# Hybrid encoder step on one core: a norm row spread by TensorE, partial sums of squares added in PSUM, half factors written directly, and a longer planned delay for two w_o loads

## Chip, cores and metric

The kernel runs on one core of one Trainium2 chip. The metric is the device time of one execution in microseconds (us); the figure quoted is the median of several runs.

## The reference

One layer of a streaming encoder for 1024 prompt frames and 32 sample frames (1056 in all), width 1024:

```
h = rmsnorm(x, g_norm);  z = h @ w_in                  # 1024 x 8192
o_a = differential attention(q, k, v of z);  o_r = retention(q, k, v of z)
x = x + (sigmoid(g_a) * o_a + sigmoid(g_r) * o_r) @ w_o          # 1024 x 1024
x = x + (silu(h2 @ w_ff_gate) * (h2 @ w_ff_up)) @ w_ff_down      # h2 = rmsnorm(x), d_ff = 2816
x = x + sigmoid(rmsnorm(x) @ w_ple_gate) * (p @ w_ple)
```

All large products are computed from two f16 parts per operand (a high and a low part, three matmuls per product), so each weight block has to be scaled by a power of two and split into its parts on the chip before TensorE can use it.

## The kernel before

**Stages.** First the eight heads: for each head two weight pairs (A and B, each made of two 256-column blocks of w_in), and for each of nine row tiles of 128 frames a projection, attention and retention (functions `project`, `unit_a`, `unit_b`). Then the product with w_o, the second norm, and the gate/up products over 22 blocks of 128 columns (`load_gu`, `gu_pair`, `gu_sums`), which use a seven-product scheme. Then the down projection (`load_dn`, later `load_dn_now`) and the last gate.

**Order of the work.** A planner (`Flow`) runs at build time. Generators yield estimated costs per engine (M is TensorE, V VectorE, S ScalarE, G GpSimd, D the DMA), waits and delays; the planner simulates the engines by these estimates and emits instructions in the order of its simulated times. On the chip each engine then works through its own list strictly in that order. An estimate changes nothing about an instruction, only its place in the lists. The planner has no view of the real times.

**A weight block's scale.** `load_block_steps` (w_in, w_o), `load_gu` and `load_dn` load a block into a staging tile. For the blocks concerned here, ScalarE squares it in two instructions (L416, L1615, L1668), each leaving one sum per partition; VectorE adds the two sums into a bf16 tile `wamh` (L430, L1619, L1671); TensorE adds over the partitions with a matrix of ones (one column, L300, in `weight_scale`); VectorE makes the scale `s` (L230, L234, L315, L317) and the un-scale `d` (L323). ScalarE and VectorE then write the two parts (L462 and L464; L1587 and L1590). For gate/up blocks VectorE also writes a column of `rf` (L1624) and half of `d`, `hd` (L1626), which the tanh in `gu_out` reads as its scale.

**The start.** `const_a` loads the gain columns, `const_c` the identity and ones matrices, `norm_x(i)` row tile i of x, `load_w(0, 0, ...)` the first two weight blocks, each in four pieces, and `const_g` the norm gains `gb`, already repeated over 128 partitions in DRAM (512 KB). `norm_x` multiplies x by its row factor and by `gb` (L683), after which TensorE transposes the tile (L693) and it is split into two f16 parts `xh`. The first projection (L719 to L721) needs tile 0 and both weight blocks. All loads are issued from the SP queue.

**w_o.** Two blocks come through `load_wo_0`, two through `load_wo_1`, which passes `late`; after each load the planner adds a fixed delay of 3.0 us before the block's reductions.

Of the kernel before, what the change touches and what calls it, by code (L numbers as in the profile page):

```python
# [11 lines left out]
F32 = mybir.dt.float32  # L12
# [37 lines left out]
def _f(x):  # L50
    return float(x)
# [7 lines left out]
def V(n, f=1.0, x=0.0):  # L59
    return {"V": 0.07 + x + f * n / 960.0}  # L60


def S(n, x=0.0):
    return {"S": 0.1 + x + n / 1200.0}
# [6 lines left out]
def M(us):  # L71
    return {"M": us}


def DM(mb):
    return {"D": mb * 2.9}
# [107 lines left out]
def kernel(  # L184
# [38 lines left out]
    def sm(n, tag, bufs=2, dt=F32):  # L223
        return small.tile([P, n], dt, tag=tag, name=tag, bufs=bufs)
# [61 lines left out]
        nc.tensor.matmul(out=pt[:, P:P + n], lhsT=ones32[0:n], rhs=row, start=True, stop=True)  # L286
        return pt[:, P:P + n]

    def weight_scale(amax, n, gi, tag, pool=True, norm=False, total=False, at_bank=None):


        p2 = sm(n, tag + "p2", 3)
        if total:
            if at_bank is None:
                yield ("wait", "id")
            key, psum = at_bank or ("o", ps_o)
            yield ("get", key)
            yield M(0.06)
            ps = psum.tile([P, 512], F32, tag=key, name="mt")[:, 0:1]
            nc.tensor.matmul(out=ps, lhsT=ones16, rhs=amax, start=True, stop=True)  # L300
            yield ("delay", 0.3 if at_bank else 0.0)
            yield from p2of(p2, ps, n, tag, norm)
            yield ("put", key)
        elif pool:
            yield G(0, 0.1)
            ar = sm(n, tag + "ar", 3)
            nc.gpsimd.partition_all_reduce(ar, amax, P, ABSMAX)
            yield from p2of(p2, ar, n, tag)
        else:
            ar = yield from spread_max(amax, n, tag, at_bank)  # L310
            yield from p2of(p2, ar, n, tag, norm)
            yield ("put", at_bank[0] if at_bank else "o")
        yield V(n)
        s = sm(n, tag + "s", 3)
        nc.vector.reciprocal(s, p2)  # L315
        yield V(n, 2.0)
        nc.vector.tensor_scalar(out=s, in0=s, scalar1=_f(2.0 ** (-52 if gi == 1 else -50)) if norm else 16384.0,  # L317
                                scalar2=None, op0=ALU.mult)
        d = sm(n, tag + "d", 6)
        if gi is None:  # L320
            nc.vector.tensor_scalar(out=d, in0=p2, scalar1=_f(2.0 ** (50 if norm else -14)), scalar2=None, op0=ALU.mult)
        else:
            nc.vector.tensor_scalar(out=d, in0=p2, scalar1=gd[:, gi:gi + 1], scalar2=_f(2.0 ** 64) if norm else 1.0,  # L323
                                    op0=ALU.mult, op1=ALU.mult)
        return s, d

# [65 lines left out]
    def load_block_steps(src, w, b, gi, tag, rowf, out, tail=False, due=None, late=None, hold=None):  # L392


        yield ("get", "st")
        st = stage()[:, 0:KD * 256].rearrange("p (k c) -> p k c", k=KD)
        if due == 0:

            for q in range(4):
                yield DM(0.25)  # L400
                nc.sync.dma_start(out=st[:, 2 * q:2 * q + 2], in_=src[:, 2 * q:2 * q + 2])
        else:
            yield DM(1.0)
            nc.sync.dma_start(out=st, in_=src)
            yield ("delay", 3.0)
        norm = rowf is None and not tail
        am4 = sm(4, "wam4", 3)
        am8 = sm(8, "wam8%d" % b, 1) if rowf is not None else None
        for q in range(4):
            if due is not None:  # L410
                yield ("prio", 2 if due - at[0] > FAR else -2)
            sq = st[:, 2 * q:2 * q + 2]
            if norm:
                if q % 2:
                    yield S(1024, 0.24)
                    nc.scalar.activation(w[:, 2 * q - 2:2 * q + 2, 1, 256 * b:256 * b + 256].bitcast(BF16),  # L416
                                         st[:, 2 * q - 2:2 * q + 2], AF.Square, accum_out=am4[:, q // 2:q // 2 + 1])
                continue
            yield V(512)
            if rowf is None:  # L420
                nc.vector.tensor_reduce(out=am4[:, q:q + 1], in_=sq, axis=AX.XY, op=ALU.max, apply_absolute_value=True)
            else:
                nc.vector.tensor_reduce(out=am8[:, 2 * q:2 * q + 2], in_=sq, axis=AX.X, op=ALU.max, apply_absolute_value=True)
        if rowf is not None:
            yield V(8)
            nc.vector.tensor_tensor(out=am8, in0=am8, in1=rowf, op=ALU.mult)
        yield V(4)
        am = sm(1, "wamh" if norm else "wam", 3, BF16 if norm else F32)
        if norm:
            nc.vector.tensor_tensor(out=am, in0=am4[:, 0:1], in1=am4[:, 1:2], op=ALU.add)  # L430
        else:
            nc.vector.tensor_reduce(out=am, in_=am4 if rowf is None else am8, axis=AX.X, op=ALU.max)
        s, d = yield from weight_scale(am, 1, gi, tag + str(b), tail, norm, norm)
        out[b] = d
        if rowf is not None:
            yield V(8)
            sk = sm(KD, "wsk%d" % b, 1)
            nc.vector.tensor_scalar(out=sk, in0=rowf, scalar1=s, scalar2=None, op0=ALU.mult)
        if late is not None:
            w = yield from late()  # L440
        if hold is not None:
            hold.update(st=st, sk=sk)
            return
        yield from split_block(w, b, st, s, None if rowf is None else sk, due)
# [40 lines left out]
    with ExitStack() as pa:  # L485
# [71 lines left out]
        def const_c():  # L557

            yield DM(0.2)
            nc.sync.dma_start(out=cst_sb, in_=cst)  # L560
            yield ("delay", 2.0)
            yield ("set", "id")
            yield ("wait", ("x", 0))
            yield V(P)
            nc.vector.tensor_copy(id16, id32)

        def const_g():

            yield DM(0.5)
            nc.sync.dma_start(out=gb, in_=gbc)  # L570
            yield ("delay", 2.0)
            yield ("set", "gb")

        def const_b():
# [80 lines left out]
        def norm_x(i):  # L655

            R = P if i < NT - 1 else TS
            if i > 2:
                yield ("wait", ("x", i - 3))
            if i > 3:  # L660
# [694 lines left out]
        def stream():  # L1355

            env, wAs, wBs = {}, {0: []}, {}
            flow.add(const_a(), 0)
            flow.add(const_c(), 0)
            flow.add(norm_x(0), 0)  # L1360
            load_w(0, 0, wAs[0], 0, True)
            flow.add(const_g(), 0)
            flow.add(const_b(), 0)
            for i in range(1, NT):
                flow.add(norm_x(i), 0)
# [71 lines left out]
        return psb.tile([P, 512], F32, tag="ps", name="ps")[:, 0:CH]  # L1437

    rf = const.tile([P, NF], F32, name="rf")

# [5 lines left out]
    with ExitStack() as pc:  # L1448
# [18 lines left out]
        with ExitStack() as pw:  # L1467
# [130 lines left out]
            def load_gu(j):  # L1598
# [10 lines left out]
                w = wt[:, 0:n].rearrange("p (i a k c) -> p i a k c", i=7, a=2, k=HK)  # L1609
                tmp = wt[:, n:n + 2 * HK * P].bitcast(F32).rearrange("p (k c) -> p k c", k=HK)  # L1610
                q1, q2, q3, q4 = (st[:, i * HK:(i + 1) * HK, u] for u in range(2) for i in range(2))
                am2 = sm(2, "gam2", 3)
                for i in range(2):
                    yield S(1024, 0.3)
                    nc.scalar.activation(w[:, S3 + i].bitcast(BF16), st[:, i * HK:(i + 1) * HK].rearrange("p k u c -> p u k c"),  # L1615
                                         AF.Square, accum_out=am2[:, i:i + 1])
                yield V(1)
                am = sm(1, "wamh", 3, BF16)
                nc.vector.tensor_tensor(out=am, in0=am2[:, 0:1], in1=am2[:, 1:2], op=ALU.add)  # L1619
                yield ("delay", 1.5)  # L1620
                s, d = yield from weight_scale(am, 1, 1, "gu", norm=True, total=True, at_bank=("ps", psb) if j < 4 else ("ss", pss))

                yield V(1, 1.0, 0.2)
                nc.vector.tensor_scalar(out=rf[:, j:j + 1], in0=d, scalar1=_f(2.0 ** 38), scalar2=d, op0=ALU.mult, op1=ALU.mult)  # L1624
                hd = sm(1, "hdg", 6)
                nc.vector.tensor_scalar(out=hd, in0=d, scalar1=0.5, scalar2=None, op0=ALU.mult)  # L1626
                gus[j] = w, hd
                yield ("set", ("hd", j))
                flow.add(split(j, w, s, A1, q1), 1)
                flow.add(split(j, w, s, A2, q2), 1)  # L1630
# [15 lines left out]
            def load_dn(m):  # L1646

                half = NF // 2
                sts, ams = [], sm(2, "dam", 3)
                yield ("wait", ("hd", NF - 1))  # L1650
                for b in range(2):
                    yield ("get", "st")
                    st = stage()[:, 0:half * P].rearrange("p (j c) -> p j c", j=half)
# [11 lines left out]
                w = wtile().rearrange("p (a j c) -> p a j c", a=3, j=NF)  # L1665
                for b, (st, js) in enumerate(sts):
                    yield S(half * P, 0.3)
                    nc.scalar.activation(w[:, 1, js].bitcast(BF16), st, AF.Square, accum_out=ams[:, b:b + 1])  # L1668
                yield V(2)
                am = sm(1, "wamh", 3, BF16)  # L1670
                nc.vector.tensor_tensor(out=am, in0=ams[:, 0:1], in1=ams[:, 1:2], op=ALU.add)  # L1671
                s, d = yield from weight_scale(am, 1, None, "dn", norm=True, total=True, at_bank=("ss", pss))
                for st, js in sts:
                    yield S(half * P, 0.18)
# [370 lines left out]
```

## Time and profile before

| | |
|---|---|
| median of 3 runs | 1919.94 us (1919.64 to 1921.41) |
| profiled execution, its own time | 1921.23 us |
| its span (first to last instruction) | 1919.5 us |
| granted TensorE clock, mean | 0.996 of 2.4 GHz |
| TensorE busy | 1859.3 us, 97% of the span |
| VectorE busy | 1505.6 us, 78% |
| ScalarE, GpSimd busy | 1085.6 us (57%), 685.8 us (36%) |
| read from and written to HBM | 113.61 MB, 31.34 MB |

Times of single rows are microseconds unless marked ns. In a timeline a row's first figure is when it started, its second how long it took, and the brackets hold the idle time of its engine just before it and what ended that. A matmul's own duration contains its way through the array; in a dense stream the distance between two starts is what one costs.

### The profile page before, as it was taken

The page shows a single profiled execution, that of the slowest core. Times are in us where ns is not written, and L with a number is a line of the kernel's source. Part 1 is how long each engine was busy: PE and PEld are TensorE (multiplying, and loading weights), DVE is VectorE, ACT ScalarE, POOL GpSimd, SP SyncE. Part 2 cuts the span into 40 slices and gives each one's busy share as a digit, 9 for nine tenths or more (in the row PEclk, how much of TensorE's full clock was granted, in tenths as well). Part 3 has the DMA queues.
Part 4 walks back from the last instruction along what each step waited for, and adds up shares of the span by engine and source line. Part 5 has one row for each costly group of instructions (what it writes and reads, how often), then busy time and mean ns, then how long its engine had stood idle before and what let it go on. Part 6 is the DMA issues. An engine that isn't in the chain of part 4 may idle for free.

```text
span 1919.5 us, 38340 instructions
## 1 busy us (share of the span) xinstructions
PE 1859.3 (97%) x14179; PEld 1217.1 (63%) x14179; DVE 1505.6 (78%) x3950; ACT 1085.6 (57%) x2856; POOL 685.8 (36%) x1172
## 2 busy tenths in 40 slices
PE   5899999999999999999999997999999999999999
PEld 3465565555655556655556685777777776666665
DVE  6887788888777787877887589999999986654364
ACT  6777667677676776766656345555655552111132
POOL 2655445444454444544442067232323200000010
PEclk9999999999999999999999999999999999999999
DMA  5222112112021121211214620222121117112031
GB/s 199 70 74 76 63 28 64 57 52 78 18 83 56 32 84 33 77 60 28 84 36 175 234 66 31 101 79 90 56 67 48 63 48 267 61 61 78 12 133 50
DMA packets 71948, 147.43 MB, mean 77 GB/s; under 512 B 25264, under 2 KB 52016, under 8 KB 63824
## 3 DMA queue, kind: packets, MB, share of 16 engines
q1 hardware_dynamic: 71760, 144.98, 22.6%
q8 instruction: 111, 1.82, 0.4%
q14 instruction: 77, 0.63, 0.1%
HBM read 113.61 MB, written 31.34 MB: 76 GB/s over the span
## 4 chain that ended last, share of the span: by engine, by line
PE 72%; DVE 14%; POOL 6%; ACT 4%; issue 2%; DMA 1%; SPq 0%; POOLq 0%; DVEq 0%; ACTq 0%
PE ps L471 9%; PE ps L472 9%; PE ps L473 9%; PE pj L719 7%; PE pj L721 7%; PE pj L720 7%; PE ps L1463 4%; PE ps L1462 4%; PE ps L1461 4%; PE sc L860 1%; PE sc L863 1%; DVE w L464 1%; ACT p L880 1%; DVE nm L870 1%; PE t L909 1%
## 5 line engine op out<-in xcount | busy, mean ns | idle before, releaser
L720 PE MATMUL pj<-w,xh 128*128 128x512 f16 x1024 | 389.5, 380 | 0.0
L719 PE MATMUL pj<-w,xh 128*128 128x512 f16 x1024 | 389.5, 380 | 0.0
L721 PE MATMUL pj<-w,xh 128*128 128x512 f16 x1024 | 389.4, 380 | 0.0
L472 PE MATMUL ps<-mixs,w 128*128 128x352 f16 (+1 forms) x960 | 260.9, 277 | 2.4 <-POOL mixs L1486 2.4
L471 PE MATMUL ps<-mixs,w 128*128 128x352 f16 (+1 forms) x960 | 261.0, 277 | 0.3 <-ACT pws L1339 0.3
L473 PE MATMUL ps<-mixs,w 128*128 128x352 f16 (+1 forms) x960 | 261.0, 277 | 0.0
L471 PEld LDWEIGHTS <-w 128*128 128x128 f16 x1728 | 169.8, 98 | 58.7 <-issue 5.0
L473 PEld LDWEIGHTS <-w 128*128 128x128 f16 x1728 | 169.6, 98 | 56.6 <-issue 5.6
L472 PEld LDWEIGHTS <-w 128*128 128x128 f16 x1728 | 169.6, 98 | 50.4 <-issue 1.5
L721 PEld LDWEIGHTS <-xh 128*128 128x128 f16 x1024 | 100.4, 98 | 121.8 <-issue 1.7
L1595 POOL TENSOR_TENSOR st<-st 128x512 f32<-128x512 f32 x66 | 86.2, 1305 | 250.8 <-DVE w L1590 186.6
L719 PEld LDWEIGHTS <-xh 128*128 128x128 f16 x1024 | 101.5, 99 | 76.0 <-issue 1.7
L720 PEld LDWEIGHTS <-xh 128*128 128x128 f16 x1024 | 100.4, 98 | 73.3 <-issue 1.1
L472 PE MATMUL ps<-tT,w 128*128 128x352 f16 (+1 forms) x528 | 143.6, 277 | 2.9 <-DVE tT L1486 2.9
L880 ACT ACTIVATE p<-sc,nb,scs 128x256 f32<-128x256 f32 (+7 forms) x128 | 106.5, 833 | 69.5 <-POOL nb L872 41.5
L473 PE MATMUL ps<-tT,w 128*128 128x352 f16 (+1 forms) x528 | 143.5, 277 | 0.0
L471 PE MATMUL ps<-tT,w 128*128 128x352 f16 (+1 forms) x528 | 143.5, 277 | 0.0
L1590 DVE SCALAR_TENSOR_TENSOR w<-st,gus,w 128x512 f16<-128x512 f32 x132 | 141.5, 1073 | 0.0
L870 DVE TENSOR_REDUCE nm<-sc 128x1 f32<-128x768 f32 (+6 forms) x112 | 102.9, 918 | 23.4 <-PE sc L863 22.0
L1463 PE MATMUL ps<-a,w 128*128 128x352 f16 x312 | 97.5, 313 | 0.5 <-DVE w L1681 0.5
L1462 PE MATMUL ps<-a,w 128*128 128x352 f16 x312 | 97.5, 313 | 0.0
L1461 PE MATMUL ps<-a,w 128*128 128x352 f16 x312 | 97.5, 312 | 0.0
(428 smaller groups left out, 4872.7 us busy)
## 6 DMA issues: line engine op xcount, KB each, us to landing
st<-in_win_dram SPq DMA_DIRECT2D x30, 1024.0 KB, 4.9
st<-in_wgu_dram SPq DMA_DIRECT2D x22, 1024.0 KB, 4.9
st<-in_wdn_dram SPq DMA_DIRECT2D x16, 704.0 KB, 4.2
out_dram<-kv SPq DMA_DIRECT2D x64, 128.0 KB, 1.7
a_d<-a SPq DMA_DIRECT2D x9, 528.0 KB, 2.7
b<-a_d SPq DMA_DIRECT2D x9, 528.0 KB, 7.4
mixs<-mix_d SPq DMA_DIRECT2D x8, 528.0 KB, 6.6
pw_d<-pws SPq DMA_DIRECT2D x12, 352.0 KB, 5.3
```

The costliest lines, as they stand in the source:

```text
L471: nc.tensor.matmul(out=ps, lhsT=wh, rhs=ah, start=first, stop=False)
L472: nc.tensor.matmul(out=ps, lhsT=wh, rhs=al, start=False, stop=False)
L473: nc.tensor.matmul(out=ps, lhsT=wl, rhs=ah, start=False, stop=last)
L719: nc.tensor.matmul(out=ps, lhsT=xhi, rhs=w[:, k, 0], start=(k == 0), stop=False)
L720: nc.tensor.matmul(out=ps, lhsT=xhi, rhs=w[:, k, 1], start=False, stop=False)
L721: nc.tensor.matmul(out=ps, lhsT=xh[:, k, 1, t0:t0 + P], rhs=w[:, k, 0], start=False, stop=(k == KD - 1))
L870: nc.vector.tensor_reduce(out=nm[0:R, mc], in_=pv, axis=AX.X, op=ALU.max, negate=True)
L880: nc.scalar.activation(pt[0:R, 0:NK], ps[0:R, p0:p0 + NK], AF.Exp, bias=nb[0:R, m:m + 1], scale=sc_ap[0:R], accum_out=Z[0:R, m:m + 1])
L1461: nc.tensor.matmul(out=ps, lhsT=wt[:, 0, j], rhs=a[:, 0, cs], start=(first and j == js[0]), stop=False)
L1462: nc.tensor.matmul(out=ps, lhsT=wt[:, 1, j], rhs=a[:, 0, cs], start=False, stop=False)
L1463: nc.tensor.matmul(out=ps, lhsT=wt[:, 2, j], rhs=a[:, 1, cs], start=False, stop=(last and j == js[-1]))
L1590: nc.vector.scalar_tensor_tensor(out=w[:, i, 1], in0=src, scalar=s, in1=w[:, i, 0], op0=ALU.mult, op1=ALU.subtract)
```

## The change

- `const_g` loads one row of the norm gains (4 KB) instead of 128, and TensorE spreads it over the partitions with two f32 matmuls of 512 columns by a row of ones; ScalarE copies each result into `gb`. It is handed to the planner ahead of `norm_x(0)`.
- The pieces of the second first-head weight block wait for those of the first in the plan, and the x tiles after the first wait for the second block's pieces.
- The VectorE addition of the two partial sums is gone: TensorE takes both as two accumulating one-column matmuls, reading the upper half of each f32 as bf16. This concerns 32 blocks of w_in, 22 of gate/up and 2 of down.
- For gate/up blocks L323 writes half of the un-scale directly into a column of a common tile `hds`; the `rf` columns are computed by one instruction for all 22 blocks, at the first down block, from `hds`.
- After a load that carries `late` (two blocks of w_o) the planned delay is 9.0 us instead of 3.0.

```diff
-            nc.tensor.matmul(out=ps, lhsT=ones16, rhs=amax, start=True, stop=True)
+            top = amax.bitcast(BF16).rearrange("p (c t) -> p c t", t=2)
+            for i in range(2):
+                nc.tensor.matmul(out=ps, lhsT=ones16, rhs=top[:, i:i + 1, 1], start=(i == 0), stop=(i == 1))
...
-        d = sm(n, tag + "d", 6)
+        half = d is not None
+        if not half:
+            d = sm(n, tag + "d", 6)
...
-            nc.vector.tensor_scalar(out=d, in0=p2, scalar1=gd[:, gi:gi + 1], scalar2=_f(2.0 ** 64) if norm else 1.0,
+            nc.vector.tensor_scalar(out=d, in0=p2, scalar1=gd[:, gi:gi + 1], scalar2=_f(2.0 ** (63 if half else 64)) if norm else 1.0,
...
+            if b:
+                yield ("wait", "wl0")
             for q in range(4):
                 yield DM(0.25)
                 nc.sync.dma_start(out=st[:, 2 * q:2 * q + 2], in_=src[:, 2 * q:2 * q + 2])
+            yield ("set", "wl%d" % b)
...
-            yield ("delay", 3.0)
+            yield ("delay", 3.0 if late is None else 9.0)
...
-            nc.vector.tensor_tensor(out=am, in0=am4[:, 0:1], in1=am4[:, 1:2], op=ALU.add)
+            am = am4
...
-            yield DM(0.5)
-            nc.sync.dma_start(out=gb, in_=gbc)
+            yield DM(0.03)
+            nc.sync.dma_start(out=gb[0:1], in_=gbc[0:1])
             yield ("delay", 2.0)
+            yield ("wait", "id")
+            for j in range(2):
+                js = slice(512 * j, 512 * j + 512)
+                yield ("get", "o")
+                yield M(0.9)
+                pt = ps_o.tile([P, 512], F32, tag="o", name="t")
+                nc.tensor.matmul(out=pt, lhsT=ones32[0:1], rhs=gb[0:1, js], start=True, stop=True)
+                yield S(512)
+                nc.scalar.copy(gb[:, js], pt)
+                yield ("put", "o")
...
+            if i:
+                yield ("wait", "wl1")
...
+            flow.add(const_g(), 0)
             flow.add(norm_x(0), 0)
             load_w(0, 0, wAs[0], 0, True)
-            flow.add(const_g(), 0)
...
-                am = sm(1, "wamh", 3, BF16)
-                nc.vector.tensor_tensor(out=am, in0=am2[:, 0:1], in1=am2[:, 1:2], op=ALU.add)
...
-                yield V(1, 1.0, 0.2)
-                nc.vector.tensor_scalar(out=rf[:, j:j + 1], in0=d, scalar1=_f(2.0 ** 38), scalar2=d, op0=ALU.mult, op1=ALU.mult)
-                hd = sm(1, "hdg", 6)
-                nc.vector.tensor_scalar(out=hd, in0=d, scalar1=0.5, scalar2=None, op0=ALU.mult)
-                gus[j] = w, hd
+                gus[j] = w, d
...
-                yield ("wait", ("hd", NF - 1))
+                if m == 0:
+                    yield ("wait", ("hd", NF - 1))
+                    yield V(NF)
+                    nc.vector.scalar_tensor_tensor(out=rf, in0=hds, scalar=_f(2.0 ** 40), in1=hds, op0=ALU.mult, op1=ALU.mult)
```

## Rows read from the trace of the kernel before

**Rows 1.** The page's first part: busy time, share of the span, instructions.
```profile
PE 1859.3 (97%) x14179; PEld 1217.1 (63%) x14179; DVE 1505.6 (78%) x3950; ACT 1085.6 (57%) x2856; POOL 685.8 (36%) x1172
```

**Rows 2.** Windows: length, each engine's busy time, granted clock, DMA share, GB/s.
```profile
0.00:23.30 23.30, 4.08 (x17) 3.14 (x18) 10.73 (x39) 13.76 (x23) 4.43 (x15) 1.00 0.73 247
23.30:75.00 51.70, 44.41 (x235) 23.66 (x232) 46.41 (x122) 35.35 (x92) 32.37 (x57) 0.93 0.40 136
...
1090.00:1250.00 160.00, 144.78 (x1309) 113.03 (x1308) 144.73 (x301) 83.55 (x190) 85.97 (x85) 0.98 0.18 64
1250.00:1600.00 350.00, 350.00 (x3106) 269.19 (x3104) 329.81 (x734) 197.95 (x409) 88.57 (x65) 1.00 0.22 74
```

**Rows 3.** Timeline of the start: begin, duration, engine, line, operation.
```profile
6.61 0.33 SPq L570 DMA_DIRECT2D w<-in_gbc_dram  x1
...
8.23 0.21 DVE L680 TENSOR_SCALAR xrg<-xnr,gsc 128x1 f32<-128x1 f32 x1 [1.27 <-POOL xnr L755]
...
9.22 1.06 ACT L416 ACTIVATE w<-st 128x1024 bf16<-128x1024 f32 x1 [2.15 <-DMA st<-in_win_dram]
...
12.21 1.06 ACT L416 ACTIVATE w<-st 128x1024 bf16<-128x1024 f32 x1 [0.81 <-DMA st<-in_win_dram]
...
14.28 1.28 DVE L683 SCALAR_TENSOR_TENSOR w<-w,xrg 128x1024 f32<-128x1024 f32 x1 [0.72 <-DMA w<-in_gbc_dram]
...
15.62 1.12 PE L693 MATMUL t<-cst_sb,w 128*128 128x128 f32 x4 [1.85 <-DVE w L683]
...
16.24 0.72 ACT L462 ACTIVATE w<-st,A0s 128x512 f16<-128x512 f32 x1 [1.84 <-DVE A0s L317]
...
23.32 0.63 PE L719 MATMUL pj<-w,xh 128*128 128x512 f16 x1
```

**Rows 4.** Copies and casts of line 388: duration ns min/median/max.
```profile
L388 ACT CAST xh<-t x12: 557/585/585, 21.4 to 70.9; 128x512 f16<-128x512 f32 x12
```

**Rows 5.** Waits of TensorE: waiter, releaser, us in total, times, longest.
```profile
PE t L693 <- DVE w L683: 9.4, 4, 4.7
PE mt L300 <- DVE wamh L430: 7.8, 1, 7.8
PE mt L300 <- DVE wamh L1619: 7.2, 5, 3.1
PE ps L472 <- DVE tT L1486: 2.9, 1, 2.9
```

**Rows 6.** Weight loads of line 300: duration ns min/median/max.
```profile
L300 PEld LDWEIGHTS <-cst_sb x56: 96/98/151, 5.8 to 1600.2; 128*128 128x128 bf16 x56
```

**Rows 7.** Timeline of TensorE around one L300 in a dense stretch.
```profile
1297.88 0.31 PE L473 MATMUL ps<-tT,w 128*128 128x352 f16 x1
1298.03 0.17 PE L300 MATMUL mt<-wamh,cst_sb 128*128 128x1 bf16 x1
1298.06 0.24 PE L471 MATMUL ps<-mixs,w 128*128 128x176 f16 x1
```

**Rows 8.** Timeline around two of the five stalls before L300.
```profile
1153.55 0.19 ACT L1615 ACTIVATION_READ_ACCUMULATOR w<-st 128x1 f32 x1
...
1154.64 0.16 PE L300 MATMUL mt<-wamh,cst_sb 128*128 128x1 bf16 x1 [3.07 <-DVE wamh L1619]
...
1204.76 0.19 ACT L1615 ACTIVATION_READ_ACCUMULATOR w<-st 128x1 f32 x1
...
1206.53 0.16 PE L300 MATMUL mt<-wamh,cst_sb 128*128 128x1 bf16 x1 [2.06 <-DVE wamh L1619]
```

**Rows 9.** VectorE groups, 1060 to 1600 us: count, busy us, mean ns, idle before.
```profile
L1624 DVE TENSOR_SCALAR rf<-gud 128x1 f32<-128x1 f32 x22 | 4.6, 207 | 0.0
...
L1619 DVE TENSOR_TENSOR wamh<-gam 128x1 bf16<-128x1 f32 x22 | 4.4, 199 | 0.0
...
L1626 DVE TENSOR_SCALAR hdg<-gud 128x1 f32<-128x1 f32 x22 | 3.2, 144 | 0.0
```

**Rows 10.** Timeline at the second late w_o block.
```profile
1055.43 0.69 DVE L423 TENSOR_REDUCE wam<-st 128x2 f32<-128x512 f32 x1 [1.21 <-DMA st<-in_wo_dram]
```

More of the change, by code (lines that the diff above doesn't have):

```diff
@@ L287, in spread_max, with weight_scale @@
         return pt[:, P:P + n]
-    def weight_scale(amax, n, gi, tag, pool=True, norm=False, total=False, at_bank=None):
+    def weight_scale(amax, n, gi, tag, pool=True, norm=False, total=False, at_bank=None, d=None):
         p2 = sm(n, tag + "p2", 3)
@@ L404, in load_block_steps @@
             nc.sync.dma_start(out=st, in_=src)
-            yield ("delay", 3.0)
+            yield ("delay", 3.0 if late is None else 9.0)
         norm = rowf is None and not tail
-        am4 = sm(4, "wam4", 3)
+        am4 = sm(2, "wamh", 3) if norm else sm(4, "wam4", 3)
         am8 = sm(8, "wam8%d" % b, 1) if rowf is not None else None
@@ L426, in load_block_steps @@
             nc.vector.tensor_tensor(out=am8, in0=am8, in1=rowf, op=ALU.mult)
-        yield V(4)
-        am = sm(1, "wamh" if norm else "wam", 3, BF16 if norm else F32)
         if norm:
-            nc.vector.tensor_tensor(out=am, in0=am4[:, 0:1], in1=am4[:, 1:2], op=ALU.add)
+            am = am4
         else:
+            yield V(4)
+            am = sm(1, "wam", 3)
             nc.vector.tensor_reduce(out=am, in_=am4 if rowf is None else am8, axis=AX.X, op=ALU.max)
@@ L1439 @@
     rf = const.tile([P, NF], F32, name="rf")
+    hds = const.tile([P, NF], F32, name="hds")
     HK = KD // 2
@@ L1611, in load_gu @@
                 q1, q2, q3, q4 = (st[:, i * HK:(i + 1) * HK, u] for u in range(2) for i in range(2))
-                am2 = sm(2, "gam2", 3)
+                am = sm(2, "gam2", 3)
                 for i in range(2):
@@ L1615, in load_gu @@
                     nc.scalar.activation(w[:, S3 + i].bitcast(BF16), st[:, i * HK:(i + 1) * HK].rearrange("p k u c -> p u k c"),
-                                         AF.Square, accum_out=am2[:, i:i + 1])
-                yield V(1)
-                am = sm(1, "wamh", 3, BF16)
-                nc.vector.tensor_tensor(out=am, in0=am2[:, 0:1], in1=am2[:, 1:2], op=ALU.add)
+                                         AF.Square, accum_out=am[:, i:i + 1])
                 yield ("delay", 1.5)
-                s, d = yield from weight_scale(am, 1, 1, "gu", norm=True, total=True, at_bank=("ps", psb) if j < 4 else ("ss", pss))
-                yield V(1, 1.0, 0.2)
-                nc.vector.tensor_scalar(out=rf[:, j:j + 1], in0=d, scalar1=_f(2.0 ** 38), scalar2=d, op0=ALU.mult, op1=ALU.mult)
-                hd = sm(1, "hdg", 6)
-                nc.vector.tensor_scalar(out=hd, in0=d, scalar1=0.5, scalar2=None, op0=ALU.mult)
-                gus[j] = w, hd
+                s, d = yield from weight_scale(am, 1, 1, "gu", norm=True, total=True, at_bank=("ps", psb) if j < 4 else ("ss", pss),
+                                               d=hds[:, j:j + 1])
+                gus[j] = w, d
                 yield ("set", ("hd", j))
@@ L1648, in load_dn @@
                 half = NF // 2
-                sts, ams = [], sm(2, "dam", 3)
-                yield ("wait", ("hd", NF - 1))
+                sts, am = [], sm(2, "dam", 3)
+                if m == 0:
+                    yield ("wait", ("hd", NF - 1))
+                    yield V(NF)
+                    nc.vector.scalar_tensor_tensor(out=rf, in0=hds, scalar=_f(2.0 ** 40), in1=hds, op0=ALU.mult, op1=ALU.mult)
                 for b in range(2):
@@ L1667, in load_dn @@
                     yield S(half * P, 0.3)
[L1668 to L1671, printed above, removed]
+                    nc.scalar.activation(w[:, 1, js].bitcast(BF16), st, AF.Square, accum_out=am[:, b:b + 1])
                 s, d = yield from weight_scale(am, 1, None, "dn", norm=True, total=True, at_bank=("ss", pss))
```

## The prediction

> **What bounds the kernel now.** I read the page's first part first: TensorE is busy 97% of the span [rows 1], so work taken from another engine pays only where TensorE stands idle at that moment, and each matmul added in a dense stretch is paid in full. Next I split the span into windows and took busy from length, to see where the idle time is [rows 2]: 19.2 us lie before 23.3 us, 7.3 us between 23.3 and 75, 15.2 us between 1090 and 1250, and none at all between 1250 and 1600. The rest (1919.5 - 1859.3 = 60.2, less these 41.7) is spread over the other 1,330 us. So a change to the loading of weights can gain in two places, the start and the entry to the gate/up stage, and can only cost in between.
>
> The timeline of the start tells what sets the first projection [rows 3]. The row factor of x tile 0 is ready at 8.44 (8.23 + 0.21), yet L683 starts at 14.28, released by the load of `gbc`, which was issued at 6.61 behind eight pieces of weights. Until 15.56 this long VectorE instruction stands ahead of the small ones that make the first weight scale; the first split on ScalarE, at 16.24, was released by that scale. The first projection starts at 23.32.
>
> The list of TensorE's waits names the second place [rows 5]: L300 waits five times, 7.2 us in all, for the VectorE addition `wamh` in the gate/up stage. The timeline around two of them shows that the addition's inputs were long there [rows 8]: ScalarE had its sums at 1153.74 and 1204.95, TensorE went on at 1154.64 and 1206.53. The addition stood in a VectorE list that is 90% busy in this window [rows 2].
>
> **The change part by part.** *The gain row.* It removes a 512 KB load ahead of L683. In its place stand a 4 KB load issued early, two matmuls and two copies. A price for a 512-column f32 matmul is not in the trace; the nearest row is four f32 transposes of 128 columns, together 512, in 1.12 us in the same unwarmed stretch [rows 3], so about 1.1 us each, between 0.6 (half, if it streamed at the higher of the two clock levels, which this stretch did not see) and 2.2 (double, should a product cost more than a transpose). A copy of 512 columns out of PSUM takes 0.585 us on ScalarE [rows 4]. Begun with the ones matrix, before 5 us, that is 2 x (1.1 + 0.6) = 3.4, ready near 8.5, just when the row factor is. TensorE and ScalarE are nearly empty then (4.08 and 13.76 of 23.3 us busy [rows 2]), so it costs nothing but a possible delay of the small matmuls for the gain scale, about 1 us. L683 then starts at 8.5 to 10.5 in place of 14.28.
>
> *The order of the first weights.* Now the pieces alternate between the blocks: the first square waits until 9.22, for the third piece, the third square until 12.21, for the seventh [rows 3], 0.75 us a piece. With block 0's four pieces first, its last one lands near 10.0, its second square ends near 11.2 instead of 13.3, and its scale is no longer behind L683: ready near 12.5 instead of 16.2. Block 1's last piece, the eighth, lands near 13.0; square 1.25, scale 1.2, split and low part 1.5 give a first projection near 17, 6.3 us before today's. That is the upper end. What is kept depends on the next 50 us: there VectorE is busy 46.41 of 51.70 us and TensorE waits 7.3 us [rows 2]. VectorE, not TensorE, is close to the limit there; its heavy work begins some 5 us earlier, but it will stand idle between L683 and the first low part for 2 us or so, and ScalarE has 1.2 us more to do. I take 4.3 of the 6.3, bounds 1 and 7 (the upper by one of the waits in the window falling away).
>
> *Sums added by TensorE.* 56 more one-column matmuls, each with its own load of the ones. In a dense stretch L300 moves the next start by 0.03 us (1298.03 to 1298.06) [rows 7], so 56 x 0.028 = 1.6 us. The other bound is that the second weight load (98 ns [rows 6]) is not covered by a long matmul ahead of it: 56 x 0.126 = 7.1 us. I take 1.6, because the existing weight load after L300 has no more cover than the new one will have and shows none of those 98 ns in the distance of starts. The Trainium skill, page "TensorE: Matmul & The Clock Gate", section "Back-to-back issue gap", speaks against so low a price: it gives short matmuls about 25 ns when decoded in hardware but about 62 ns when decoded by the sequencer, and by the latter the 56 would cost 3.5 us; the 28 ns of the row side with the former.
>
> Against it stand the stalls before L300. Without the addition TensorE waits for ScalarE's sums alone: at 1154.64 some 0.8 us less, at 1206.53 some 1.5 less, and the three others (7.2 - 3.07 - 2.06 = 2.1) could go. That makes up to 4.4 us. But behind the first two stalls TensorE waits 2.9 us for a difference tile made by VectorE [rows 5], and what is saved ahead of it is given back there unless VectorE is earlier too. VectorE loses 199 + 207 + 144 = 550 ns per gate/up block [rows 9], 1.6 us for the first three. The granted clock is 0.98 of the window's 160 us [rows 2], so some 6 us ran at 1.2 GHz, after the long stalls; a shorter stall could give 1 to 2 us of that back. I take a gain of 2.5, bounds 0 and 6. In the head stage the 32 additions cost nothing to anyone at present, except that the first is part of the 7.8 us start wait [rows 5], counted above.
>
> *Half factors, `rf` in one.* This takes work only from VectorE. From 1250 to 1600 TensorE is never idle [rows 2], so the other 19 blocks' 10 us of VectorE time gain nothing. The single `rf` instruction (some 0.2 us by its like [rows 9]) comes ahead of the first down block. Zero, up to 0.3 either way.
>
> *The delay of w_o.* One VectorE reduction of the second late block stood 1.21 us at the head of its queue, waiting for its load [rows 10]. Placed 6 us later in the plan it would find its data there. TensorE lost at most this time to it. I take 0.4, bounds -1 (the later block in turn late) and 1.2.
>
> **Sum.** Against the profiled execution's 1921.2 us: -4.3 - 2.5 - 0.4 + 1.6 = -5.6. The profile lies 1.3 above the median of the runs; against the median 1919.94 that makes 1914.3 us.
>
> **Rivals.** *The start is swallowed.* VectorE and the chains through GpSimd set the end of the first 75 us whatever the first projection does. For it: VectorE's 46.41 of 51.70 us [rows 2]. Against it: that work starts earlier as well. With only 1 us kept: -1 - 2.5 - 0.4 + 1.6 = -2.3, 1917.6 us.
>
> *The stalls move.* The time saved before L300 is given back at the wait for the difference tile and after. For it: VectorE 144.73 of 160 us [rows 2]. Against: two of the five stalls lie later. With 0.5 kept: -4.3 - 0.5 - 0.4 + 1.6 = -3.6, 1916.3 us.
>
> *Both in full.* -6.3 - 6 - 0.4 + 1.6 = -11.1, 1908.8 us.
>
> *Slower: the plan puts sums too early.* Without the VectorE addition and its queue, the planner thinks a block's sum ready earlier and puts L300 nearer to ScalarE's squares. If the real squares are later than planned, TensorE stands before L300 as at 1154.64, 3.07 us, plus some 1.5 us of low clock after it: 4.6 each. From two new stalls on the gain is gone, from four it is slower: -5.6 + 4 x 4.6 = +12.8, 1932.7 us. Against it: in the steady stretch there is no idle before any L300 from 1250 to 1600.
>
> **Chances.** Forecast 0.50; swallowed start 0.20; moved stalls 0.14; both in full 0.08; sums too early 0.08. A measurement of this kernel can tell about 0.2%, 3.8 us, from no change: faster means below 1916.1. The forecast and the full case lie there, and a little of the moved stalls; the swallowed start and most of the moved stalls lie within; faster 0.61, same 0.31, slower 0.08. The range that leaves out the full case's far part and the slower one is 1909.5 to 1919.5.
>
> **What would show it.** Right: L683 starts before 10.5 us and the first L719 before 20; the TensorE idle time before 75 us falls from 26.5 to about 22; no `wamh` wait remains and TensorE's idle time from 1090 to 1250 falls from 15.2 to 12 or less, with the stalls before L300 ended by ScalarE; two L300 in a row start some 28 ns apart. Wrong: the first L719 starts early but idle time from 23 to 75 us grows by as much; longer waits for difference tiles; new idle time before L300 after 1250; or distances of 0.1 us between the two one-column matmuls.

## The result and the profile after

The changed kernel takes 1923.63 us (median of 18 runs, 1921.92 to 1927.19) against 1920.18 (18 runs, 1919.19 to 1922.28) for the kernel before: ratio 1.0018, interval 1.0012 to 1.0024. It is 3.5 us slower, not 5.6 faster. The time lies outside the forecast range. The profiled execution took 1923.85, its span 1922.0.

The page's first part after, against [rows 1]: 60 more matmuls (56 halves of sums and two 512-column products, each of which counts as two), 10.6 us more TensorE busy time, 7.4 less on VectorE.

```profile
PE 1869.9 (97%) x14239; PEld 1220.4 (63%) x14239; DVE 1498.2 (78%) x3827; ACT 1085.7 (56%) x2864; POOL 697.3 (36%) x1190
```

The windows of [rows 2] after (length, busy time and count of TensorE, its weight loads, VectorE, ScalarE and GpSimd, then clock, DMA share, GB/s):

```profile
0.00:23.30 23.30, 13.16 (x37) 6.08 (x38) 13.96 (x47) 16.10 (x28) 6.07 (x17) 1.00 0.70 228
23.30:75.00 51.70, 44.66 (x263) 24.91 (x262) 48.22 (x132) 39.42 (x108) 32.99 (x57) 0.93 0.40 137
...
1090.00:1250.00 160.00, 144.56 (x1320) 113.98 (x1319) 136.66 (x275) 82.97 (x188) 85.72 (x85) 0.97 0.19 65
1250.00:1600.00 350.00, 349.65 (x3118) 268.99 (x3116) 332.06 (x694) 195.05 (x411) 88.93 (x65) 1.00 0.21 72
```

Idle TensorE time before 75 us fell from 26.5 to 10.1 + 7.0 = 17.2, where about 22 was forecast; between 1090 and 1250 it is 15.4 where it was 15.2. Idle time does not show the loss: over the whole span it fell from 60.2 to 52.1 us while the kernel became slower. The progress of the work does. These are the rows of the first projection product, whose matmuls run through the whole head stage, before and after (duration in ns min/median/max, then first and last start in us):

```profile
L719 PE MATMUL pj<-w,xh x1024: 376/379/634, 23.3 to 1031.0; 128*128 128x512 f16 x171
L740 PE MATMUL pj<-w,xh x1024: 376/379/634, 16.9 to 1032.6; 128*128 128x512 f16 x171
```

The first starts 6.4 us earlier than before, the last 1.6 us later. So the lead is lost, and more than that, in the heads, where the prediction did not look.

The timeline of the start after answers to [rows 3]:

```profile
1.64 0.33 SPq L579 DMA_DIRECT2D w<-in_gbc_dram  x1
...
4.10 2.07 PE L587 MATMUL t<-w,cst_sb 1*128 1x512 f32 x2
...
5.97 0.42 PE L286 MATMUL mt<-gmr,cst_sb 3*128 3x3 f32 x2
...
10.27 1.28 DVE L704 SCALAR_TENSOR_TENSOR w<-w,xrg 128x1024 f32<-128x1024 f32 x1 [1.05 <-ACT w L589]
...
16.93 0.58 PE L740 MATMUL pj<-w,xh 128*128 128x512 f16 x1 [1.90 <-ACT w L471]
```

L704 (the old L683) starts at 10.27 where 8.5 to 10.5 was forecast, and the first projection at 16.93 where 17 was: 6.4 us earlier than before.

TensorE's waits after, against [rows 5]: the 7.8 and 7.2 us before L300 (now L303) are 4.0 and 2.6 and end with ScalarE, as forecast. But 9.5 us now go to the difference tile `mixs`.

```profile
PE ps L481 <- DVE mixs L1508: 9.5, 2, 8.5
PE mt L303 <- ACT w L425: 4.0, 3, 1.5
...
PE sc L881 <- ACT q L393: 2.8, 2, 2.6
PE mt L303 <- ACT w L1637: 2.6, 2, 2.2
```

And one pair of sums in the dense stretch after, where [rows 7] showed a single one:

```profile
1298.92 0.31 PE L482 MATMUL ps<-mixs,w 128*128 128x352 f16 x1
...
1299.07 0.19 PE L303 MATMUL mt<-gam,cst_sb 128*128 128x1 bf16 x2
...
1299.12 0.31 PE L480 MATMUL ps<-tT,w 128*128 128x352 f16 x1
```

The pair moves the next start by 0.05 us where one moved it by 0.03. Over all sums that nothing held up, the median distance to the next start is 0.054 us for the pair (52 of 56) and 0.028 for the single one (55 of 56).

### The profile page after: what moved, and what is told of

Same layout as the page of the kernel before. It is cut to its first block, busy times and chain, and to the rows that moved or that the text cites. A ratio compares the mean times of both kernels' runs of the same rounds, so it can differ in the third digit from the quotient of the medians.

```text
span 1922.0 us, 38381 instructions
## 1 busy us (share of the span) xinstructions
PE 1869.9 (97%) x14239; PEld 1220.4 (63%) x14239; DVE 1498.2 (78%) x3827; ACT 1085.7 (56%) x2864; POOL 697.3 (36%) x1190
## 4 chain that ended last, share of the span: by engine, by line
PE 77%; DVE 11%; POOL 4%; ACT 4%; issue 2%; DMA 1%; SPq 0%; POOLq 0%; ACTq 0%; DVEq 0%
PE ps L480 9%; PE ps L481 9%; PE ps L482 9%; PE pj L740 8%; PE pj L741 8%; PE pj L742 8%; PE ps L1483 4%; PE ps L1484 4%; PE ps L1485 4%; PE sc L881 1%; PE t L930 1%; DVE w L473 1%; PE sc L884 1%; PE pj L751 1%; DVE nm L891 1%
## 5 line engine op out<-in xcount | busy, mean ns | idle before, releaser
L1617 POOL TENSOR_TENSOR st<-st 128x512 f32<-128x512 f32 x66 | 93.6, 1418 | 238.8 <-ACT w L1637 129.0
L891 DVE TENSOR_REDUCE nm<-sc 128x2 f32<-128x256 f32 (+6 forms) x112 | 102.9, 918 | 36.3 <-PE sc L884 35.7
L1609 ACT ACTIVATE w<-st,gus 128x512 f16<-128x512 f32 x132 | 88.5, 714 | 50.5 <-DVE gus L320 47.1
L1612 DVE SCALAR_TENSOR_TENSOR w<-st,gus,w 128x512 f16<-128x512 f32 x132 | 104.5, 795 | 0.7 <-ACT w L1609 0.7
L1485 PE MATMUL ps<-a,w 128*128 128x352 f16 x312 | 97.5, 313 | 0.0
L1484 PE MATMUL ps<-a,w 128*128 128x352 f16 x312 | 97.5, 313 | 0.0
## 6 DMA issues: line engine op xcount, KB each, us to landing
st<-in_win_dram SPq DMA_DIRECT2D x30, 1024.0 KB, 4.9
st<-in_wgu_dram SPq DMA_DIRECT2D x22, 1024.0 KB, 5.1
```

The source lines that it names most:

```text
L891: nc.vector.tensor_reduce(out=nm[0:R, mc], in_=pv, axis=AX.X, op=ALU.max, negate=True)
L1484: nc.tensor.matmul(out=ps, lhsT=wt[:, 1, j], rhs=a[:, 0, cs], start=False, stop=False)
L1485: nc.tensor.matmul(out=ps, lhsT=wt[:, 2, j], rhs=a[:, 1, cs], start=False, stop=(last and j == js[-1]))
L1612: nc.vector.scalar_tensor_tensor(out=w[:, i, 1], in0=src, scalar=s, in1=w[:, i, 0], op0=ALU.mult, op1=ALU.subtract)
L1617: nc.gpsimd.tensor_tensor(out=out, in0=in0, in1=in1, op=op)
```

## The experiments

The theories: **A**, the removed estimates (a removed VectorE addition also removes its `yield V(...)` from the planner's input) make the planner write another, worse order of the lists; **B**, the added matmuls and the direct wait for ScalarE cost more on the chip than forecast; **C**, the earlier start itself worsens the heads; **D**, the half factors or the later w_o loads cost it. Expectations of later runs use also **S**: the time depends smoothly on the size of the estimate. "Before" ran at 1920.2 to 1920.5 beside all of them. All kernels are the kernel before, or after, with the edit shown.

### One part at a time

*The start alone* (the hunks of `const_g`, `wl0`/`wl1` and the order of `flow.add`).

> The kernel before with the start's part alone (gain row spread by TensorE, first block's pieces before the second's, later x tiles behind them). Theory A (order): the loss after 260 us comes from the instruction order that the planner makes once the additions are gone from its plan; then this part keeps its lead of 4.6 to 5.9 us to the end: about 1915 us. Theory B (cost): the loss comes from what the added matmuls and the direct wait for ScalarE cost on the chip: also about 1915. Theory C (start): the earlier start itself makes the order of the heads worse; then the lead at 260 us is 5 and at 1060 us it is below 0: 1920 to 1924 us.

1914.74 us, ratio 0.997 (0.9958 to 0.9982): 5.6 us faster, 4.3 forecast.

*The sums alone*, with the estimates of the removed additions gone:

```diff
-        yield V(4)
...
-            nc.vector.tensor_tensor(out=am, in0=am4[:, 0:1], in1=am4[:, 1:2], op=ALU.add)
+            am = am4
```

> The kernel before with the sums alone (VectorE addition gone, two one-column matmuls). Theory A (order): stalls of the head stage from 260 to 1060 us grow by about 5 us, 1.4 us for the matmuls, the gate/up entry about even: 1923 to 1929 us. Theory B (cost): the same time, from the same part. Theory C (start): no head loss; 1917 to 1921 us.

1917.03 us, ratio 0.9985 (0.9977 to 0.9994): 3.3 us faster.

*The half factors alone* (`hds`, one `rf` instruction).

> The kernel before with the half factors and the single rf instruction alone. By the prediction's step nothing up to 0.3 us either way: 1919.5 to 1921 us. Rival: with another plan from the gate/up stage on, the wait for the difference tile of the last chunk changes: as the changed kernel's 8.5 us of idle time at 1197 us stands in its own trace, 3 to 5 us slower, 1923 to 1925.

1918.89 us, ratio 0.9991 (0.9982 to 0.9999): 1.6 us faster.

*The later w_o loads alone.*

```diff
-            yield ("delay", 3.0)
+            yield ("delay", 3.0 if late is None else 9.0)
```

> The kernel before with the planned delay of 9.0 us for the two late w_o blocks alone; TensorE's list changes in some 20 rows. Prediction's step: 0.4 us faster, bounds 1.2 faster and 1 slower: 1919 to 1921.5 us. Rival: the later reductions now come late for the second w_o pair and TensorE waits at the head of the w_o product, as for 1.8 us at 1058 us in the changed kernel: 1921.5 to 1923 us.

1923.1 us, ratio 1.0012 (1.0003 to 1.0022): 2.6 us slower. The waits around w_o in this run, and its window from 1030 to 1090:

```profile
PE mt L275 <- DVE wam L432: 0.6, 1, 0.6
PE ps L471 <- DVE o1c L230: 0.6, 1, 0.6
PE mt L286 <- DVE o1mc L278: 0.4, 1, 0.4
PE mt L286 <- DVE o0mc L278: 0.4, 1, 0.4
```
```profile
1030.00:1090.00 60.00, 57.80 (x429) 38.61 (x428) 33.67 (x100) 29.08 (x70) 4.08 (x9) 0.97 0.85 294
```

and the same window of the kernel before:

```profile
1030.00:1090.00 60.00, 58.52 (x446) 39.48 (x445) 34.48 (x102) 29.18 (x70) 4.26 (x9) 1.00 0.85 296
```

Waits in front of the small w_o matmuls come one after another; idle time grows by 0.7 us, and the granted clock is 0.97 where it had been 1.00, up to 60 x 0.03 = 1.8 us more. Together that is at most 2.5, near the 2.6 measured.

By the four parts taken alone the change should be -5.6 - 3.3 - 1.6 + 2.6 = -7.9. It is +3.5. So no part is the culprit by itself, and B, C and D in their simple form fall. So does A in its simple form: it had put the sums alone at 1923 to 1929, and they took 1917.03. The half factors alone met neither of their two expectations. What is left of A is that the parts together make an order that none of them makes alone.

### The same instructions in two orders

*Sums by TensorE, planner still told of the additions*: the estimates stay with no instruction behind them.

```diff
         if norm:
+            yield V(4)
             am = am4
```

(and likewise `yield V(1)` and `yield V(2)` for gate/up and down)

> As the run with the sums alone, but the planner still counts the removed additions (the estimate stays, no instruction stands behind it), so every other instruction keeps its place in its list. Theory A (order): no head loss; 1.4 us for the matmuls, and up to 4.4 us of the five stalls in the gate/up stage gained: 1916 to 1921 us, below the run with the sums alone by 4 us or more. Theory B (cost): as the run with the sums alone, within 1.5 us.

1920.59 us, ratio 1.0001 (0.9993 to 1.001): no difference. TensorE's and GpSimd's lists are then row for row those of before, the second halves of the sums aside. So at an unchanged order the sums by TensorE changed the time by 0.2 us (interval -1.3 to +1.9), and nearly all of the 3.3 us of the sums alone came from the new order.

*The opposite*: the additions stay on VectorE, the planner no longer counts them.

```diff
-        yield V(4)
+        if not norm:
+            yield V(4)
```

(`yield V(1)`, `yield V(2)` removed likewise)

> The kernel before with every instruction of before, but the planner no longer counts the 56 additions (they are still issued, at the place where the last square ends in the plan). Theory A (order): slower by the head loss alone, 4 to 8 us: 1924 to 1928 us. Theory B (cost): nothing added on the chip, so no loss: 1919 to 1921 us.

1925.0 us, ratio 1.0025 (1.0016 to 1.0034): 4.8 us slower. Its TensorE, ScalarE and GpSimd lists are those of the sums alone, which took 1917.03, but for the sums themselves. An order planned without the additions is 8 us slower when VectorE still has to make them.

*Start and sums together*, with the planner's new order and with the old one:

> Start and sums together, without the half factors and without the longer w_o delay; TensorE's list for the heads is that of the changed kernel, row for row. Theory A (order: the two parts together make another plan of the heads than either alone, and that plan is the bad one): the lead over the kernel before is 5 to 6 us at 260 us and between -1 and -3 at 1010 us; 1920 to 1925 us. Theory D (the loss comes from the half factors or the w_o delay): the lead at 1010 us stays above 3; 1912 to 1916 us.

> The same two parts with the same instructions, but the planner still counts the removed additions, so TensorE's list is that of the run with the start alone, row for row, with a second one-column matmul at each sum. Theory A: it keeps the start's lead; 1.4 us for the matmuls, up to 2.5 us of stalls in the gate/up stage gained: 1912 to 1916 us, and below the other run of these two parts by 6 us or more. Theory B (start and sums together cost this time on the chip, whatever the order): within 2 us of the other run.

1925.14 us (ratio 1.0025, 1.0016 to 1.0034) and 1913.06 us (0.9964, 0.9951 to 0.9977). These two run the same arithmetic side by side on one chip; they differ only in what the planner was told of 56 small VectorE additions that neither makes. (The planner also picks the engine of some elementwise work, so the slow one has 29 more instructions on GpSimd and 29 fewer on VectorE.) That is worth 12.1 us. The slow one's lists equal those of the changed kernel through the whole head stage; the fast one's TensorE list is that of the start alone, to which it adds a gain of 1.7 us (1914.74 to 1913.06) by the sums themselves, within the intervals of both. The page rows of the slow and of the fast one:

```profile
PE 1872.1 (97%) x14239; PEld 1221.0 (63%) x14239; DVE 1502.0 (78%) x3870; ACT 1087.9 (57%) x2863; POOL 694.8 (36%) x1191
```
```profile
PE 1860.7 (97%) x14239; PEld 1218.5 (64%) x14239; DVE 1497.5 (78%) x3899; ACT 1090.2 (57%) x2863; POOL 679.5 (36%) x1162
```

11.4 of the 12.2 us between their spans (1923.4 and 1911.2) stand as TensorE *busy* time at the same 14,239 instructions. Two things are in it. One is the clock: the slow kernel's TensorE is busy for 15.9 us of stretches granted 0.50 (57.6 to 64.4, 1170.4 to 1177.2 and 1207.9 to 1211.3 us), the fast one's for 6.8 (1149.0 to 1152.4, 1155.8 to 1159.2); at twice the clock these would take half, so up to 4.6 us of the 11.4 are the clock. The other is short stalls: a matmul's duration holds its way through the array [rows 7], so a stall shorter than that leaves no idle time in the profile. The starts show them. From 80 us to the last projection matmul, at a granted clock of 1.00 in both, the next start follows a projection matmul (duration 379 ns, some 2,910 of them) after 220.2 ns on average in the slow kernel and 218.4 in the fast one, which makes 5.2 us; after a transpose of `qst` (402 of them) it is 66.3 against 59.5 ns, 2.8 us; other products give back a part. The Trainium skill, page "Trainium Kernel Development and Optimization", section "Performance Expectations", warns that matmul busy time is a bad metric for how close a kernel is to roofline, because matmuls are pipelined; these two rows agree in that the slower kernel is the busier one.

The last start of the first projection product places the loss in the heads:

| run | first start, us | last start, us | time, us |
|---|---|---|---|
| before | 23.3 | 1031.0 | 1920.2 to 1920.5 |
| start alone | 17.9 | 1024.0 | 1914.74 |
| sums alone | 23.3 | 1022.6 | 1917.03 |
| sums, estimates kept | 22.9 | 1030.8 | 1920.59 |
| additions kept, estimates gone | 22.9 | 1031.0 | 1925.0 |
| start and sums | 17.1 | 1032.2 | 1925.14 |
| start and sums, estimates kept | 18.3 | 1023.8 | 1913.06 |

8.4 of the 12.1 us between the last two are there when the heads end.

### The changed kernel with the old order of the heads

*One line put back in the changed kernel*, the estimate for the 32 w_in additions:

```diff
         if norm:
+            yield V(4)
             am = am4
```

> The changed kernel with one line more: in the blocks of w_in the planner still counts the removed addition (0.07 us and a hand-over), so TensorE's list for the heads is that of the run with the start alone, row for row. Every instruction of the changed kernel is there. Theory A (order of the heads): the lead at the start of the w_o product is 5 or more in place of -3; 1913 to 1917 us, 7 to 10 us below the changed kernel. Theory D (gate/up or w_o set the end): within 3 us of the changed kernel, 1921 to 1925.

1916.61 us, ratio 0.998 (0.9971 to 0.9989): 7.0 us faster than the changed kernel by one line that issues no instruction. The long gate/up stall is as it was in the changed kernel, so it is not what differs:

```profile
PE ps L480 <- DVE mixs L1507: 9.5, 2, 8.5
```

But the projection of the heads ends at 1023.1 us, where it ended at 1032.6:

```profile
L739 PE MATMUL pj<-w,xh x1024: 376/379/632, 17.8 to 1023.1; 128*128 128x512 f16 x171
```

So the loss of the heads is gone, all 9.5 us of it, and some 2.5 are given back behind them.

The progress of the first projection product, one of whose matmuls is issued for each us or so of the heads (1,024 in 1,008 us): length of the window, TensorE time in that line and its count, clock, DMA share, GB/s. Before:

```profile
0.00:256.00 256.00, 87.16 (x226) 0.99 0.28 91
256.00:600.00 344.00, 136.38 (x360) 1.00 0.18 56
600.00:1000.00 400.00, 155.35 (x410) 1.00 0.18 56
```

after:

```profile
0.00:256.00 256.00, 89.25 (x231) 0.99 0.28 89
256.00:600.00 344.00, 135.24 (x357) 1.00 0.18 56
600.00:1000.00 400.00, 154.22 (x407) 1.00 0.18 56
```

after with that line:

```profile
0.00:256.00 256.00, 90.11 (x235) 1.00 0.27 89
256.00:600.00 344.00, 136.91 (x361) 1.00 0.18 58
600.00:1000.00 400.00, 154.36 (x407) 1.00 0.17 54
```

The changed kernel is 5 matmuls ahead of before at 256 us, 2 at 600 and 1 behind at 1000; with the line put back it is 9, 10 and 7 ahead. By this count half of the difference is there by 256 us; by all of TensorE's matmuls it is a quarter (1637 against 1655 with the line by 256 us, 7032 against 7101 by 1000). Three windows of TensorE (the same columns) show where it starts, in the changed kernel:

```profile
52.00:56.00 4.00, 1.45 (x18) 1.00 0.21 66
56.00:60.00 4.00, 2.37 (x18) 0.57 0.10 35
60.00:64.00 4.00, 4.00 (x17) 0.57 0.84 279
```

and with the line:

```profile
52.00:56.00 4.00, 2.22 (x13) 1.00 0.09 33
56.00:60.00 4.00, 3.75 (x27) 1.00 0.93 334
60.00:64.00 4.00, 3.55 (x23) 1.00 0.47 197
```

From 52 to 56 us the changed kernel's TensorE stood idle for 2.6 us, and for 1.6 more by 60; the longest wait there is the 2.6 us before L881 listed above, for a tile `q` from ScalarE. From 56 to 64 us the granted clock is 0.57, most of it at 1.2 GHz: with 2.37 + 4.00 us busy, up to 6.37 x 0.43 = 2.7 us. In the good order the idle time is 1.8 and 0.3 us, that wait does not occur, and the clock stays at 1.00. That the wait brought the clock down is likely and not shown. Against the kernel before this stretch is no loss, since that has one like it (0.83 from 60 to 64 us, 0.50 from 64 to 68). The larger part of the loss comes after 256 us, where the clock is 1.00; it appears as no long wait but as short ones that the starts show: from 80 us on, 220.3 ns after a projection matmul against 218.5 with the line, 5.4 us in all, and 66.9 against 59.4 after a transpose of `qst`, 3.0 us.

*The same without the later w_o loads, and the changed kernel without them*: `yield ("delay", 3.0)` in both.

> As the changed kernel with the heads' plan kept, and also without the longer w_o delay. If the parts' effects add once the order of the heads is kept: start -5.6, sums -1.5 on top of it, half factors -1.6, so 1911 to 1913 us, the fastest so far, 2 to 3 us below the one with the delay. If the half factors' gain alone was the order of that plan: 1913 to 1916.

> The changed kernel without the longer w_o delay; the heads' list is the changed kernel's. If the delay costs here what it costs alone (2.6 us): 1920 to 1922 us. Rival: in this plan of the heads the blocks arrive otherwise and the delay gains what it was meant to; then slower than the changed kernel, 1924 to 1926.

1914.72 us (0.997, 0.9959 to 0.9982) and 1924.73 us (1.0023, 1.0014 to 1.0033). The 9.0 us delay costs 1.9 us in the good order, where no run of either kernel reaches into the range of the other (1915.15 to 1917.53 with it, 1913.49 to 1915.05 without). In the changed kernel it seems to save 1.1 (1923.63 against 1924.73), but the intervals of the ratios overlap. So perhaps even its sign hangs on the order around it. Of the two expectations for the good order the lower, in which all gains add, was missed: the half factors' 1.6 us is not seen on top of start and sums. It is not seen in the bad order either, where start and sums took 1925.14 and the same with the half factors 1924.73.

*A smaller estimate*: start and sums, with a third figure for the 32 additions.

```diff
         if norm:
+            yield {"V": 0.03}
             am = am4
```

> Start and sums together, with the removed addition of the w_in blocks counted in the plan at 0.03 us of VectorE time in place of 0.07, a third order of the heads that agrees with neither of the other two beyond 3% of TensorE's list; the instructions are the same. Theory A says that a tiny estimate moves the time by the order it happens to give, not in proportion: anywhere from 1911 to 1926 us, and not a point on a line between the two others. Theory S (smooth): a third to a half of the way from 1913 to 1925, 1917 to 1920 us.

1915.84 us (0.9975, 0.9965 to 0.9984), where no estimate gave 1925.14 and the full one 1913.06 (that one counts the additions of gate/up and down too, this one does not). Its TensorE list agrees with neither beyond the first 3%. It is below the range of S, and its last projection matmul starts at 1021.2 us, earlier than with the full estimate (1023.8) and with none (1032.2). So over these three points the estimate doesn't act as a cost with a slope; it looks like a throw of the dice over the whole order, though A's own range here was so wide that it could hardly miss.

The lowest median of all is that of start and sums with the old estimates, 1913.06 us, 7.4 below the kernel before and 10.6 below the changed one. Its single runs (1912.41 to 1915.88) overlap those of the start alone (1913.8 to 1915.53), so these two are not told apart.

## Why the prediction was wrong

**The start** was right in mechanism and mis-sized. Its milestones came as forecast (10.27; 16.93). Alone it gained 5.6 where 4.3 was taken, inside the bounds 1 and 7. The first of the two 512-column products cost 1.87 us (4.10 to 5.97), not 1.1, and the second lasted as long. So the gain row came at 10.2 and not near 8.5, and L704 waited 1.05 us for it; the first projection did not, since it was released by a split on ScalarE. The prediction took the start to run at the lower clock level, although the clock column of [rows 2] says 1.00 there. The starts bear it out:

```profile
23.75 0.63 PE L720 MATMUL pj<-w,xh 128*128 128x512 f16 x1
...
28.92 0.38 PE L719 MATMUL pj<-w,xh 128*128 128x512 f16 x1
29.14 0.38 PE L720 MATMUL pj<-w,xh 128*128 128x512 f16 x1
```

In the kernel before, the first 512-column matmuls stand 0.43 us apart (23.32 to 23.75), those from 28.92 on 0.22. The first clock record of this trace begins at 28.5 us, so the 1.00 before it is not a reading. Part of the gain that the sum did not have can be the clock: in the kernel before it is 0.93 from 23.3 to 75 us [rows 2], with the start alone 1.00 over the same stretch. "The start is swallowed" was wrong on the chip when the start is alone.

**The price of the added matmuls** was right: the pair moves the next start by 0.026 us more than one did (0.054 against 0.028), 56 x 0.026 = 1.5, forecast 1.6. The Trainium skill's 62 ns for a sequencer-decoded matmul (page "TensorE: Matmul & The Clock Gate", section "Back-to-back issue gap") is not what these rows show; its 25 ns is near.

**The stalls before L300** went as the rival "the stalls move" said, and further. The waits fell from 7.2 to 2.6, ended by ScalarE as at this one after:

```profile
1156.57 0.19 ACT L1637 ACTIVATION_READ_ACCUMULATOR w<-st 128x1 f32 x1
...
1156.81 0.16 PE L303 MATMUL mt<-gam,cst_sb 128*128 128x1 bf16 x1 [2.22 <-ACT w L1637]
```

but the wait for the difference tile took it all: 15.2 us idle before, 15.4 after. The 2.5 us of gain in this term is nil in the changed kernel. It is not nil in general: with the sums at the old order the same window holds 12.2 us of idle time, 3.0 less than before. The wait of 8.5 us stands only in the four kernels that have both the sums and the half factors.

**Half factors**: zero forecast, -1.6 alone, beyond the 0.3 allowed; added to start and sums, -0.4 (1925.14 to 1924.73), within noise. Most of the instructions removed lie beside a TensorE that is never idle, so the order is the likelier cause of the 1.6: it changes from the gate/up stage on. That is only argued; the old estimates were not kept in a run of this part.

**The w_o delay** had the wrong sign: -0.4 forecast, +2.6 alone. The prediction asked only whether the second late block would find its data. It did not ask what stands behind both blocks in the lists, nor what the clock does after a chain of short waits. Here no more than some 20 rows of TensorE's list moved.

**The step that failed** is the one in the part on the sums: "In the head stage the 32 additions cost nothing to anyone at present". On the chip that holds: with the old order the sums cost nothing (+0.2 us without the new start, -1.7 with it, neither clear of noise). But the additions also stood in the planner's input, and with their estimates gone the planner sorted all lists of the heads anew. The prediction priced each edit in lists that stay as they are, and so put the effect of the new order at nothing. Its slower rival looked at the planner, but only at the place of L300 itself after 1250 us, where the changed kernel is busy 349.65 of 350 us. The re-sorted heads cost 7.0 us by the one-line experiment, which turns the remaining -3.6 us into the +3.5 measured. A second, smaller step is the w_o delay, -0.4 in the sum and +1.9 with the old order of the heads. With that order and without the delay the kernel is 5.5 us faster than before, where the sum without that term says 5.2. That this agrees is partly luck, since the start gave more than its term and the stalls in front of the gate/up stage nothing.

**What stays open.** Which engine's list makes the changed order bad is not settled: TensorE, VectorE and GpSimd are sorted together. GpSimd has 1191 instructions in the slow one of the pair and 1162 in the fast one, since the planner chooses an engine for some; that goes along with the time in this pair and was not tested as its cause. The kernels with the sums alone and with the additions kept have 1158 there and lie 8 us apart. Nor was it shown why the lists planned without the additions are good with the old start (-3.3 us) and bad with the new one. That the parts do not add because each start of the plan leads to another order fits the runs, but it is an argument.

## What to carry to other kernels

Where a planner writes the order from estimates, removing an instruction is two changes: its work, and its estimate. Try the two apart (keep the estimate with nothing behind it) before judging either; here the work was worth under 2 us in an order planned with it, and the estimate up to 12. And price an edit from rows of the old trace only for as long as the lists stay as they are; past that the honest range is that of other orders of the same work, some 0.6% here.

## What the runs showed of the hardware that was not expected

A 512-column f32 matmul with one row of weights stands as two instructions in the profile and took 1.87 us at the start (4.10 to 5.97), where four f32 transposes of 128 columns had taken 1.12 together [rows 3].

A wait of 2.6 us in a thin stretch may cost more than itself: TensorE stood idle for 2.6 us between 52 and 56 us and for 1.6 more by 60, and the granted clock is 0.57 from 56 to 64, up to 2.7 us more; in the order with 1.8 and 0.3 us idle there it stayed at 1.00.

TensorE's busy time differed by 11.4 us over the same 14,239 matmuls, of which the lower clock explains at most 4.6. Short stalls can thus be missing from the list of waits while they set the time: a projection matmul lasts 379 ns and the next can start 216 ns after it, so up to 163 ns of a wait behind it leave no idle time.
